# A two-block transformer forward pass on one core: GpSimd's tile arithmetic goes to VectorE, and two prices of the list scheduler change

## The chip, the cores and the metric

The program runs on one core of one Trainium2 chip. The metric is the device time of one execution in microseconds (us). Five engines of the core take part: TensorE (PE; its weight loads stand as PEld), VectorE (DVE), ScalarE (ACT), GpSimd (POOL) and SyncE (SP), whose queue issues the weight loads from HBM.

## The reference

512 tokens of width 1024 go through two blocks of two layers each, all in float32.

```python
def first_block(...):                      # DEPTH = 2
    for layer in range(DEPTH):
        g = norm_gains[layer]
        h = rmsnorm(x, g[0])
        x = x + 0.5 * rmsnorm(swiglu(h, w_ffn_gate[layer, 0], w_ffn_up[layer, 0], w_ffn_down[layer, 0]), g[1])
        h = rmsnorm(x, g[2])
        x = x + rmsnorm(token_mixer(h, ...), g[3])         # 16 heads: dilated, differential, stick-breaking
        h = rmsnorm(x, g[4])
        x = x + 0.5 * rmsnorm(swiglu(h, w_ffn_gate[layer, 1], ...), g[5])
    return x

def second_block(x, ...):
    for l in range(DEPTH):
        proj = x @ w_in[l]
        ...
        o_a = hgrn2_mixer(hq, hf, hi, hg, lbs[l], hg_norm_w[l])     # gated recurrence, 4 heads
        o_b = nsa_mixer(nq, ...)                                    # sparse attention, 8 heads
        mix = jnp.concatenate([o_a, o_b], axis=-1) @ w_out[l]
        x = layer_norm(ALPHA * x + mix, ln1_g[l], ln1_b[l])
        ffn = (jax.nn.silu(x @ w_ffn_gate[l]) * (x @ w_ffn_up[l])) @ w_ffn_down[l]
        x = layer_norm(ALPHA * x + ffn, ln2_g[l], ln2_b[l])
    return x
```

## The kernel before

**Matmuls.** Activations lie feature by token: `x` is eight tiles of 128x512. Every large product is made of rounded matmuls (the type fp32r): a float32 operand is split into a rounded part `hi` and a rest `lo = src - hi`, and three matmuls (hi by hi, hi by lo, lo by hi) are summed in PSUM. For weights, `weights` loads a `raw` tile by SP's queue and makes two `ws` tiles from it: the `copy` to `hi` may run on VectorE or ScalarE, the subtraction for `lo` is marked `either`. Activations go through `split` in the same way (tiles `h`, `gu`, `m`).

**Stages.** A feed-forward stage runs 22 units of gate and up products (`mm<-h,ws`), then the down product (`mm<-gu,ws`); a mixer runs its own projections, heads and an output product (`mm<-m,ws`). Each stage ends in a tail (`tail` in the first block, `tail_ln` in the second), whose last units are cut into two halves of 256 tokens. When a half's units are done, `post` makes the norm: column sums on TensorE (`nb<-ones,acc`), `rsqrt` as a chain of 12 small VectorE instructions on tiles `sm`, two transposes (`nb<-c_ident,sm`) that spread the result, then for each of the eight tiles `tc<-y,nb` and `x<-x,tc`. The next stage's preparation follows: `tc<-x,c_gains`, the split to `h`, and for the norm of `x` a square on ScalarE and sums `tc<-tc`. The six such passages of the first block, and four in the second, are called transitions here. While a half is normed, TensorE works on the other half's units, and its weights need `ws` tiles from the same helper engines.

**Order.** Nothing of the order is written by hand. `Recorder` records all instructions on logical tiles; a list scheduler with prices (`Op.price`, ns) and latencies (`LAT`) simulates the five engines, in 12 rounds forward and backward, and keeps the shortest. Then `issue` emits every instruction in that order, so that each engine's queue is fixed and all instructions carry the line of `issue`, L665. An instruction marked `either` has two forms, and the scheduler picks VectorE or GpSimd for each one as it goes; `copy` and `scale` have a VectorE and a ScalarE form. `either` stands only where both operands lie in SBUF (`split` names VectorE where its source is in PSUM). A few tiles are cleared by `nc.gpsimd.memset` whatever the marks say.

Of the kernel before, what the change touches and what calls it, by code (L numbers as in the profile page):

```python
# [26 lines left out]


class Buf:
    """A logical tile. Its slot and its Tile tile come when the order of instructions is known."""  # L30

    def __init__(self, parts, cols, dt, tag, name, dram=None):
        self.parts, self.cols, self.dt, self.tag, self.name, self.dram = parts, cols, dt, tag, name, dram
# [15 lines left out]


class V:
    """A view of a logical tile: partitions, and an access pattern over a partition's elements."""

    def __init__(self, buf, dt, p0, np_, off, dims, pstep=None, raw=None):
        self.buf, self.dt, self.p0, self.np, self.off, self.dims, self.raw = buf, dt, p0, np_, off, dims, raw
# [122 lines left out]
class Op:  # L178
# [3 lines left out]
    def __init__(self, idx, eng, meth, args, kw):  # L182
        self.idx, self.eng, self.meth, self.args, self.kw = idx, eng, meth, args, kw
        vs = [x for x in args if isinstance(x, V)]
        outs = []
        ins = []
        for i, x in enumerate(args):
            if isinstance(x, V):
                (outs if i == 0 or i == 3 and meth == "pair" else ins).append(x)
        for k, x in kw.items():  # L190
            if isinstance(x, V):
                (outs if k == "accum_out" else ins).append(x)
        self.outs, self.ins = outs, ins
        self.deps, self.users = {}, []
        self.bufs = list({id(v.buf): v.buf for v in outs + ins}.values())
        self.func = args[2] if meth == "activation" and args[2] in SETS else None
        self.prices = {}
        self.forms = {}
        if meth == "copy":
            forms = {"vector": ("tensor_copy", args, kw), "scalar": ("activation", args + (AF.Copy,), kw)}  # L200
        elif meth == "scale":
            out, src, by = args
            forms = {"vector": ("tensor_scalar", (out, src, by, None), {"op0": OP.mult}),
                     "scalar": ("activation", (out, src, AF.Copy), {"scale": by})}
        else:
            forms = {e: (meth, args, kw) for e in (("vector", "gpsimd") if eng == "either" else (eng,))}
        for e in forms:
            self.eng = e
            self.meth, self.args, self.kw = forms[e]
            self.price()  # L210
            self.prices[e] = self.cost
        self.forms = forms
        self.choose(next(iter(forms)))
# [5 lines left out]
    def price(self):  # L219
        m = self.meth  # L220
        out = self.outs[0] if self.outs else None
        n = out.count() if out is not None else 0
        vs = self.ins + self.outs
        psum = any(v.buf.tag in PSUM for v in vs)
        if self.eng == "tensor":
            lhs = self.ins[0]
            load = lhs.count() / 1.2
            if lhs.dt == F32R:
                self.busy = n / 2.4
                self.cost = max(n / 2.4 + 2.5, load)  # L230
            elif m == "transpose":
                self.busy = self.cost = 107
            elif m == "pair":
                self.busy = 4 * n / 2.4
                self.cost = self.busy + 110
            else:
                self.busy = 4 * n / 2.4
                self.cost = max(self.busy + 2, 2 * load if n > 8 or n == 1 else load)
        elif self.eng == "sync":
            self.cost = max(475, vs[0].count() * vs[0].np / 90.0)  # L240
        elif self.eng == "scalar":
            self.cost = (52 if psum else 94) + n / 1.2 + (187 if "accum_out" in self.kw or isinstance(self.kw.get("bias"), V) else 0)
        elif self.eng == "gpsimd":
            self.cost = 90 + {"memset": 1.0, "tensor_copy": 3.5}.get(m, 2.22) * n
        else:
            ptr = any(v.count() == 1 for v in self.ins[1:])
            if m in ("tensor_copy", "tensor_scalar", "memset") and not psum:
                self.cost = 65 + n / 1.92 + (64 if ptr else 0)
            elif m == "reciprocal":
                self.cost = 65 + 8 * n / 0.96  # L250
            elif m == "tensor_tensor_reduce" or m == "tensor_reduce":
                self.cost = 75 + self.ins[0].count() / 0.96
            else:
                self.cost = 70 + n / 0.96 + (60 if psum and m == "scalar_tensor_tensor" else 0)
# [19 lines left out]


class Recorder:
    """Records instructions on logical tiles, orders them by a list scheduler, and issues them in that order."""

    def __init__(self, nc, tc, ctx, plan):
        self.bass_nc, self.tc, self.ctx, self.plan = nc, tc, ctx, plan  # L280
# [105 lines left out]
        return out  # L386

    def backward(self):
        """Schedules the reversed instructions, those that ended last first; the starts in forward time."""
        ops = self.ops  # L390
        engines = ("tensor", "scalar", "vector", "gpsimd", "sync")
        ready = {e: [] for e in engines}
        idle = {e: True for e in engines}
        left = [len(op.users) for op in ops]
        freed = [()] * len(ops)
        for b in self.bufs:
            if b.slot is not None and b.prior is not None and b.opener is not None:
                freed[b.opener] += tuple(b.prior.members)
                for i in b.prior.members:
                    left[i] += 1  # L400
        at = [0.0] * len(ops)
        late = [0.0] * len(ops)
        events = []
        for op in ops:
            if left[op.idx] == 0:
                heapq.heappush(ready[op.eng], (-op.end, op.idx))
        now, done = 0.0, 0
        while done < len(ops):
            for e in engines:
                if idle[e] and ready[e]:  # L410
                    i = heapq.heappop(ready[e])[1]
                    idle[e] = False
                    heapq.heappush(events, (now + ops[i].cost, 0, i))
            now, kind, i = heapq.heappop(events)
            op = ops[i]
            if kind:
                heapq.heappush(ready[op.eng], (-op.end, i))
                continue
            idle[op.eng] = True
            done += 1  # L420
            late[i] = -now
            for d in op.deps:
                left[d] -= 1
                at[d] = max(at[d], now + LAT[ops[d].eng][op.eng])
                if left[d] == 0:
                    heapq.heappush(events, (at[d], 1, d))
            for d in freed[i]:
                left[d] -= 1
                at[d] = max(at[d], now + (2000 if ops[d].eng == "sync" else 180))
                if left[d] == 0:  # L430
                    heapq.heappush(events, (at[d], 1, d))
        return late
# [1421 lines left out]
```

## Time and profile before

| | before |
|---|---|
| device time, median of 3 runs | 3787.7 us (3786.96 to 3789.73) |
| span of the profiled execution | 3776.2 us |
| median less that span | 11.5 us |
| mean granted TensorE clock | 0.978 of full speed |
| PE busy | 3631.1 us (96% of the span) |
| DVE, ACT, POOL busy | 2241.1, 1699.6, 1078.0 us |

The profiled execution has no clocked time of its own beside its span: it runs from the first to the last instruction, 3776.2 us, and the timed runs come out 11.5 us longer, which is start and end outside the span. The busy time of an engine is the union of its instructions' durations. The granted clock is 1.00 at 2.4 GHz and 0.50 at 1.2 GHz.

### The profile page before, as it was taken

To read this page: it belongs to the slowest core of one execution; us is meant where nothing else is said; L and a number is where in the kernel's file an instruction comes from. 1 tells how busy PE (TensorE), PEld (TensorE's weight loads), DVE (VectorE), ACT (ScalarE), POOL (GpSimd) and SP (SyncE) were. 2 spreads that over 40 slices of the span, in tenths; PEclk is the share of its full clock that TensorE was granted. 3 is DMA by queue.
4 is the path that set the end of the run, shared out by engine and by line. 5 is a ranking of instruction groups with operands and counts; after the bars stand their busy time and mean duration, and the time that the engine had idled before them with its cause. 6 is when DMAs were issued, how large, how long until landed. Compare 5 with 4: busy or idle time off the path is not lost.

```text
span 3776.2 us, 56593 instructions
## 1 busy us (share of the span) xinstructions
PE 3631.1 (96%) x20836; PEld 3016.9 (80%) x20836; DVE 2241.1 (59%) x4611; ACT 1699.6 (45%) x3550; POOL 1078.0 (29%) x999
## 2 busy tenths in 40 slices
PE   8999899999999999899899999999999999999998
PEld 7878877778898889767788897668888977678888
DVE  7443787764367545886844384677333766674335
ACT  5333456543344334565433354465332555654324
POOL 3220422443224211522633042334111333232112
PEclk9999999999999999999999999899999999999999
DMA  5224422232353224312322452013323531123234
GB/s 165 95 93 133 157 81 76 96 112 95 95 150 124 95 92 144 130 59 74 125 98 93 118 173 93 29 32 123 112 95 102 172 98 51 40 90 129 95 90 139
DMA packets 121622, 393.08 MB, mean 104 GB/s; under 512 B 14813, under 2 KB 20102, under 8 KB 121345
## 3 DMA queue, kind: packets, MB, share of 16 engines
q1 hardware_dynamic: 121344, 389.47, 32.6%
q8 instruction: 164, 2.69, 0.3%
q14 instruction: 114, 0.93, 0.1%
HBM read 384.65 MB, written 4.77 MB: 103 GB/s over the span
## 4 chain that ended last, share of the span: by engine, by line
PE 47%; DVE 6%; issue 1%; ACT 1%; POOL 0%; DMA 0%; ACTq 0%; DVEq 0%; POOLq 0%; SPq 0%
PE mm L665 38%; PE at L665 4%; PE ah L665 2%; PE pv L662 2%; DVE ws L665 1%; PE ah L662 1%; DVE sm L665 1%; DVE tc L665 1%; DVE hw L665 1%; DVE h L665 1%; DVE x L665 0%; PE nb L665 0%; ACT ws L665 0%; POOL ws L665 0%; ACT L659 0%
## 5 line engine op out<-in xcount | busy, mean ns | idle before, releaser
L665 PE MATMUL mm<-h,ws 128*128 128x512 f32 (+1 forms) x9792 | 2102.3, 362 | 53.9 <-DVE ws L665 16.9
L665 PEld LDWEIGHTS mm<-h,ws 128*128 128x128 f32 x9792 | 1645.8, 192 | 357.8 <-issue 25.1
L665 ACT ACTIVATE ws<-raw 128x512 fp32r<-128x512 f32 (+1 forms) x1283 | 782.0, 616 | 1417.8 <-PE mm L665 1370.8
L665 POOL TENSOR_TENSOR ws<-raw,ws 128x512 fp32r<-128x512 f32 (+1 forms) x506 | 654.5, 1295 | 2061.6 <-ACT ws L665 1592.3
L665 DVE TENSOR_TENSOR ws<-raw,ws 128x512 fp32r<-128x512 f32 (+2 forms) x926 | 682.3, 741 | 798.6 <-ACT ws L665 732.1
L665 PE MATMUL mm<-gu,ws 128*128 128x256 f32 (+1 forms) x4752 | 813.0, 323 | 11.9 <-DVE ws L665 7.3
L665 PEld LDWEIGHTS mm<-gu,ws 128*128 128x128 f32 x4752 | 692.2, 191 | 90.5 <-DVE ws L665 12.9
L665 DVE TENSOR_TENSOR te<-te,mm 128x256 f32<-128x256 f32 (+1 forms) x228 | 98.8, 460 | 279.9 <-PE mm L665 275.2
L665 PE MATMUL mm<-ws,h 128*128 128x256 f32 (+1 forms) x1344 | 254.9, 303 | 1.7 <-DVE sm L665 0.7
L665 PE MATMUL mm<-m,ws 128*128 128x256 f32 (+1 forms) x1248 | 218.3, 321 | 7.5 <-DVE ws L665 7.2
L665 PEld LDWEIGHTS mm<-ws,h 128*128 128x128 f32 x1344 | 203.2, 195 | 14.7 <-issue 6.3
L665 PEld LDWEIGHTS mm<-m,ws 128*128 128x128 f32 x1248 | 175.6, 195 | 32.3 <-issue 12.4
L665 ACT ACTIVATE row<-row,sm 128x512 f32<-128x512 f32 (+2 forms) x267 | 148.3, 572 | 58.2 <-DVE sm L665 57.2
L665 ACT ACTIVATE gu<-te 128x256 fp32r<-128x256 f32 (+1 forms) x210 | 89.5, 452 | 129.8 <-DVE te L665 118.4
L665 DVE TENSOR_TENSOR te<-te,rt 128x256 f32<-128x256 f32 x157 | 119.4, 792 | 0.5
L665 DVE CAST ws<-raw 128x512 fp32r<-128x512 f32 x149 | 97.7, 656 | 33.2 <-PE mm L665 27.7
L665 DVE TENSOR_TENSOR te<-mm,rt 128x256 f32<-128x256 f32 x176 | 67.8, 419 | 81.7 <-PE mm L665 80.4
L665 POOL TENSOR_TENSOR hw<-hw 128x256 f32<-128x256 f32 x106 | 88.7, 846 | 92.9 <-ACT hw L665 80.0
L665 PE MATMUL at<-c_ident,row 128*128 128x128 f32 x528 | 114.4, 286 | 0.4 <-DVE sm L665 0.3
L665 DVE TENSOR_TENSOR gu<-te,gu 128x256 fp32r<-128x256 f32 (+1 forms) x159 | 94.2, 611 | 30.3 <-ACT gu L665 26.0
L665 DVE CUSTOM_DVE_ANT_0 row<-at,T 128x128 f32<-128x128 f32 (+1 forms) x180 | 88.8, 509 | 25.6 <-PE at L665 23.6
L665 ACT ACTIVATE hw<-hw 128x256 f32<-128x256 f32 (+2 forms) x181 | 75.5, 456 | 55.1 <-DVE hw L665 28.1
(249 smaller groups left out, 3429.7 us busy)
## 6 DMA issues: line engine op xcount, KB each, us to landing
raw<-in_wg_dram SPq DMA_DIRECT2D x156, 512.0 KB, 3.3
raw<-in_wu_dram SPq DMA_DIRECT2D x156, 512.0 KB, 3.2
raw<-in_wd_dram SPq DMA_DIRECT2D x144, 512.0 KB, 3.5
raw<-in_wd_dram SPq DMA_DIRECT2D x72, 384.0 KB, 3.2
raw<-in_wout_dram SPq DMA_DIRECT2D x52, 512.0 KB, 3.3
raw<-in_w_f_dram SPq DMA_DIRECT2D x52, 512.0 KB, 3.4
raw<-in_win_f_dram SPq DMA_DIRECT2D x44, 512.0 KB, 3.3
raw<-in_win_v_dram SPq DMA_DIRECT2D x20, 512.0 KB, 3.2
```

The costliest lines, as they stand in the source:

```text
L662: nc.tensor.matmul(*args[0:3], **kw)
L665: r = getattr(getattr(nc, op.eng), op.meth)(*args, **kw)
```

## The change

The diff in its core (three comment strings are dropped as well, without a change of line numbers):

```diff
@@ Op.__init__ @@
         else:
-            forms = {e: (meth, args, kw) for e in (("vector", "gpsimd") if eng == "either" else (eng,))}
+            forms = {e: (meth, args, kw) for e in ("vector" if eng == "either" else eng,)}
@@ Op.price @@
             if lhs.dt == F32R:
                 self.busy = n / 2.4
-                self.cost = max(n / 2.4 + 2.5, load)
+                self.cost = max(n / 2.4 + 13, load)
...
         elif self.eng == "scalar":
-            self.cost = (52 if psum else 94) + n / 1.2 + (187 if "accum_out" in self.kw or isinstance(self.kw.get("bias"), V) else 0)
+            self.cost = (62 if psum else 106) + n / 1.2 + (187 if "accum_out" in self.kw or isinstance(self.kw.get("bias"), V) else 0)
```

An `either` instruction now has a VectorE form alone. A rounded matmul of 512 columns is priced at 226.3 ns in place of 215.8, one of 256 columns at 119.7 in place of 109.2, and a ScalarE instruction at 10 or 12 ns more. Prices set the order and the choice between VectorE and ScalarE, and no instruction's work.

In the two programs TensorE has 19692 instructions before and now, and SP 857. GpSimd goes from 1004 to 42, VectorE from 4613 to 5431, ScalarE from 3312 to 3451. Of the 962 instructions that leave GpSimd 471 are the `lo` of a 128x512 weight tile. In exchange 92 of the 145 copies `ws<-raw` that VectorE made go to ScalarE.

VectorE's queue in the transition after layer 1's mixer (the fifth of the first block, 1790 to 1860 us in the trace), from the last step of the first half's `rsqrt` on. Before:

```order
L665 SCALAR_TENSOR_TENSOR sm<-sm 128x2 x2
L665 TENSOR_TENSOR tc<-y,nb 128x256 x3
L665 TENSOR_TENSOR x_70<-x_70,tc 128x256
L665 TENSOR_TENSOR tc<-y,nb 128x256 x2
L665 TENSOR_TENSOR x_72<-x_72,tc 128x256
L665 TENSOR_TENSOR x_78<-x_78,tc 128x256
L665 TENSOR_TENSOR tc<-y,nb 128x256 x3
L665 TENSOR_TENSOR x_88<-x_88,tc 128x256
```

The same place now:

```order
L665 SCALAR_TENSOR_TENSOR sm<-sm 128x2 x2
L665 TENSOR_TENSOR ws<-raw,ws 128x512
L665 TENSOR_TENSOR acc<-acc,te 128x256
L665 TENSOR_TENSOR tc<-y,nb 128x256 x2
L665 TENSOR_TENSOR x_72<-x_72,tc 128x256
L665 TENSOR_TENSOR tc<-y,nb 128x256
L665 TENSOR_TENSOR x_74<-x_74,tc 128x256
L665 TENSOR_TENSOR x_70<-x_70,tc 128x256
L665 TENSOR_TENSOR tc<-y,nb 128x256 x2
L665 TENSOR_TENSOR x_78<-x_78,tc 128x256
L665 TENSOR_TENSOR x_76<-x_76,tc 128x256
L665 TENSOR_TENSOR tc<-y,nb 128x256 x2
```

All eight `x<-x,tc` of the half now stand in VectorE's queue, where four did, and a weight tile's `lo` and a sum `acc<-acc,te` stand between the end of `rsqrt` and the first `tc<-y,nb`.

GpSimd's queue at the same place before (`x_...` are residual tiles, `ws` weights, `h` the next stage's input):

```order
L665 TENSOR_TENSOR ws<-raw,ws 128x512 x2
L665 TENSOR_TENSOR x_74<-x_74,tc 128x256
L665 TENSOR_TENSOR x_76<-x_76,tc 128x256
L665 TENSOR_TENSOR acc<-acc,te 128x256
L665 TENSOR_TENSOR x_84<-x_84,tc 128x256
L665 TENSOR_TENSOR x_94<-x_94,tc 128x256
L665 TENSOR_TENSOR ws<-raw,ws 128x512
L665 TENSOR_TENSOR acc<-acc,te 128x256
L665 TENSOR_TENSOR h<-tc,h 128x256 x2
```

GpSimd's queue now has nothing in the whole first block after its first clears; its rows from there on begin so:

```order
L665 MEMSET misc 128x64
L665 MEMSET mean 128x128
L665 MEMSET bd 128x256 x2
L665 MEMSET hw 128x512
L665 MEMSET hw 128x256
```

What moved is every subtraction, sum and product that GpSimd shared with VectorE; the clears stay.

## Rows read from the trace of the kernel before

**Rows 1.** The page's first part: busy us, share of the span, instructions.
```profile
PE 3631.1 (96%) x20836; PEld 3016.9 (80%) x20836; DVE 2241.1 (59%) x4611; ACT 1699.6 (45%) x3550; POOL 1078.0 (29%) x999
```

**Rows 2.** Windows: stretch, us, busy us of each engine, granted clock, DMA.
```profile
410.00:490.00 80.00, 66.64 (x505) 63.66 (x505) 74.39 (x156) 41.04 (x94) 42.43 (x38) 0.96 0.45 146
...
780.00:1100.00 320.00, 319.16 (x1623) 270.46 (x1622) 147.72 (x256) 120.65 (x230) 81.09 (x70) 1.00 0.35 110
...
1790.00:1860.00 70.00, 55.38 (x401) 52.59 (x400) 63.39 (x132) 35.86 (x81) 45.28 (x44) 0.90 0.35 114
...
2310.00:2420.00 110.00, 106.25 (x677) 81.92 (x676) 62.07 (x145) 49.66 (x114) 33.92 (x42) 0.83 0.17 56
```

**Rows 3.** The chain of waits from 1790 to 1860 us, shares by line.
```profile
by line: PE mm L665 24.4%; DVE tc L665 16.1%; DVE ws L665 12.7%; DVE sm L665 12.5%; issue 9.7%; DVE x L665 6.2%; DVE h L665 4.4%; PE nb L665 4.3%; DVE te L665 3.1%; POOL ws L665 1.9%; ACT tc L665 1.3%; ACT ws L665 1.3%; DVE acc L665 1.0%; D
```

**Rows 4.** VectorE's groups, 1790 to 1860 us: busy us, mean ns | idle before.
```profile
L665 DVE TENSOR_TENSOR ws<-raw,ws 128x512 fp32r<-128x512 f32 x16 | 13.4, 842 | 0.8 <-ACT ws L665 0.7
L665 DVE SCALAR_TENSOR_TENSOR sm<-sm 128x2 f32<-128x2 f32 x18 | 7.0, 387 | 0.6
...
L665 DVE TENSOR_TENSOR x<-x,tc 128x256 f32<-128x256 f32 x8 | 5.7, 720 | 0.0
L665 DVE TENSOR_TENSOR tc<-tc 128x256 f32<-128x256 f32 x7 | 5.4, 776 | 0.1
L665 DVE TENSOR_TENSOR h<-tc,h 128x256 fp32r<-128x256 f32 x10 | 5.4, 543 | 0.1
L665 DVE CAST ws<-raw 128x512 fp32r<-128x512 f32 x8 | 5.2, 650 | 0.9 <-PE mm L665 0.9
L665 DVE TENSOR_SCALAR tc<-x,c_gains 128x256 f32<-128x256 f32 x5 | 4.3, 869 | 0.0
L665 DVE TENSOR_TENSOR sm<-sm 128x2 f32<-128x2 f32 x10 | 3.4, 340 | 0.3
L665 DVE CAST h<-tc 128x256 fp32r<-128x256 f32 x5 | 3.1, 615 | 0.1
L665 DVE TENSOR_SCALAR sm<-sm 128x2 int32<-128x2 int32 x8 | 2.2, 278 | 0.2
```

**Rows 5.** GpSimd's largest group in the same stretch.
```profile
L665 POOL TENSOR_TENSOR ws<-raw,ws 128x512 fp32r<-128x512 f32 x16 | 21.7, 1360 | 11.2 <-ACT ws L665 6.7 <-DVE sm L665 3.0 <-DVE ws L665 1.0
```

**Rows 6.** VectorE's groups from 1400 to 1450 us, where GpSimd does nothing.
```profile
L665 DVE TENSOR_TENSOR ws<-raw,ws 128x512 fp32r<-128x512 f32 x18 | 12.5, 692 | 32.2 <-ACT ws L665 31.3 <-PE mm L665 0.9
```

**Rows 7.** Timeline near 1800 us: start us, length us, engine, instruction, count.
```profile
1799.36 0.16 DVE L665 TENSOR_TENSOR sm<-sm 128x2 f32<-128x2 f32 x1
1799.55 1.41 DVE L665 SCALAR_TENSOR_TENSOR sm<-sm 128x2 f32<-128x2 f32 x2
1799.64 1.30 POOL L665 TENSOR_TENSOR ws<-raw,ws 128x512 fp32r<-128x512 f32 x1 [0.55 <-ACT ws L665]
...
1803.74 1.08 DVE L665 TENSOR_TENSOR tc<-y,nb 128x256 f32<-128x256 f32 x3 [0.59 <-PE nb L665]
...
1812.17 0.28 DVE L665 CAST h<-tc 128x256 fp32r<-128x256 f32 x1
1812.48 0.42 DVE L665 TENSOR_TENSOR h<-tc,h 128x256 fp32r<-128x256 f32 x1
```

**Rows 8.** TensorE's waits over the span: total us, times, longest us.
```profile
PE mm L665 <- DVE ws L665: 31.3, 35, 5.2
PE nb L665 <- DVE sm L665: 27.9, 17, 3.8
```

**Rows 9.** Groups of the whole span: the products of the gated recurrence (hw).
```profile
L665 POOL TENSOR_TENSOR hw<-hw 128x256 f32<-128x256 f32 x104 | 85.4, 829 | 91.2 <-ACT hw L665 80.0 <-DVE hw L665 7.7 <-DVE sm L665 1.4
...
L665 DVE TENSOR_TENSOR hw<-hw 128x256 f32<-128x256 f32 x88 | 51.9, 605 | 9.2 <-ACT hw L665 6.5 <-POOL hw L665 2.4
```

**Rows 10.** TensorE's timeline in a feed-forward stretch.
```profile
849.73 25.57 PE L665 MATMUL mm<-h,ws 128*128 128x512 f32 x110
```

## The prediction

> **What bounds the kernel now.** I read the shares first. TensorE is busy for 96% of the span and GpSimd for 29% [rows 1], so only TensorE's 145 us without work (3776.2 - 3631.1), and what it loses to a low clock, are to be had. Next come the windows [rows 2]. In the feed-forward stretch from 780 to 1100 us TensorE is busy for 319 of 320 us while GpSimd works 81 us: what GpSimd does there is hidden, and will be hidden on VectorE too, which is busy for 148 of 320. In the transitions it is the other way round. From 1790 to 1860 us TensorE is idle for 14.6 of 70 us, the granted clock is 0.90, and VectorE is busy for 63.4. Five such stretches (410 to 490, 680 to 780, 1100 to 1170, 1510 to 1570, 1790 to 1860; the first and the last stand in the rows) hold 64 us of the 145.
>
> Then the chain of waits in that stretch [rows 3]: lines of DVE make up 56% of it, PE's matmuls 24%, GpSimd 2%. TensorE's own waits over the span say the same [rows 8]: 31.3 us for `ws` tiles that VectorE ends and 27.9 us for the `rsqrt` chain. So VectorE's queue paces the transitions, and the question is whether it becomes longer or shorter.
>
> Last, why VectorE is busy there. The reader is to compare one form in two places. A `ws<-raw,ws` of 128x512 takes 692 ns where GpSimd is silent [rows 6] and 842 ns in the transition [rows 4]. A step on 128x2 `sm` takes 0.16 us alone; two of them take 1.41 us when GpSimd's 1.30 us instruction starts 0.09 us behind them [rows 7]. The means in the transition, 387 and 340 ns for `sm`, 720 for `x<-x,tc`, 869 for `tc<-x,c_gains` [rows 4], are mixtures of clean and held-up ones. VectorE is held up by GpSimd, and GpSimd needs 1360 ns for what VectorE does in 692 [rows 5, 6].
>
> A page of the Trainium skill gives this a mechanism: "SBUF — State Buffer", section "SBUF: two separate sides", says that VectorE and GpSimd share one pair of SBUF ports as an exclusive lock, taken for a whole instruction by a GpSimd operation or by a VectorE one with two SBUF inputs or in a two-port mode. By that rule all held-up time goes with GpSimd's work, and the sum below would stand as it is. The trace agrees as far as the `sm` steps beside GpSimd's 1.30 us go.
>
> **The change, part by part: VectorE's load.** I work it out for 1790 to 1860 us.
>
> Held-up time that goes, count by mean [rows 4] less clean duration ([rows 6] for 512 columns, [rows 7] for the others; I take 0.42 us for every 256-column form and for the 512-column CAST, which is kind, since a 256-column CAST takes 0.28): `ws` 16 x (842 - 692) = 2.4 us; `sm` steps 18 x (387 - 160) = 4.1, 10 x (340 - 160) = 1.8, 8 x (278 - 160) = 0.9; `x` 8 x 300 = 2.4; `tc` 7 x 356 = 2.5; `h` 10 x 123 = 1.2; CAST of `ws` 8 x 230 = 1.8; `tc<-x,c_gains` 5 x 449 = 2.2; CAST of `h` 5 x (615 - 280) = 1.7. Sum 21.0 us.
>
> Work that comes: GpSimd has 44 instructions there [rows 2], 16 of them on 512 columns [rows 5], the other 28 on 256. In a queue without waits three 256-column instructions take 1.08 us, and one alone 0.42, so each more costs 0.33 [rows 7]. A 512-column one costs 0.69 less the same overlap of 0.09, so 0.60. 16 x 0.60 + 28 x 0.33 = 18.8 us.
>
> Work that leaves VectorE for ScalarE: the order after has none of the 8 CASTs of `ws` in this transition, 8 x 0.33 = 2.6 us. ScalarE is busy for 36 of 70 us there and takes them.
>
> Net: 63.4 - 21.0 + 18.8 - 2.6 = 58.6 us, so VectorE's queue is 4.8 us shorter although it has GpSimd's work too. Five transitions: **24 us**. If the chain were on VectorE for its 56% alone, 13; if all held-up time on it went and the moved work found gaps, up to TensorE's whole idle time in the five, 64.
>
> **The clock.** At 0.90 over 70 us TensorE ran 14 us at its lower level of 1.2 GHz (2 x 0.10 x 70) [rows 2], after pauses on VectorE. Over the span 0.978 makes 166 us at half speed, at most 83 us lost. Of that I give the transitions back **12 us**: fewer pauses, not none. Bounds: 0 and 83.
>
> **The gated recurrence.** From 2310 to 2420 us the clock is 0.83, 37 us at half speed [rows 2]. There products of `hw` stand between an exponential and small matmuls. GpSimd's 104 take 829 ns, VectorE's 88 take 605, a clean one 420 [rows 9, 7]: 104 x 0.41 + 88 x 0.19 = 59 us of latency shorter. TensorE has other matmuls to run meanwhile, so I let a quarter count: **15 us**. Bounds: 0 and 59.
>
> **The prices.** They change the order alone. 110 rounded matmuls of 512 columns take 25.57 us, 232 ns each [rows 10]; the old price was 215.8, the new one is 226.3. The old plan thus expected TensorE sooner than it came, and knew nothing of held-up instructions, so its order in the transitions fits the chip badly. The new plan errs less. The price of this I know from no row. In the feed-forward stretches TensorE has some 1 us of idle time in 320 [rows 2], so there is nothing to win and little to lose; in the transitions it may be worth as much as the held-up time, or cost it. I take **10 us** gained, bounds -20 and +40.
>
> **What may get worse on the path.** The first half's `rsqrt` now has a `ws` and an `acc` between its end and the first `tc<-y,nb`, 0.60 + 0.33 us; the queue was idle for 0.59 us there while TensorE made the transposes [rows 7], so 0.3 us are left, in a handful of places. A queue that holds everything also waits as one: while VectorE waits for ScalarE's `hi`, the `x` sums behind it wait too, which GpSimd did before. That belongs to the third rival. The 42 clears left on GpSimd cost nothing I can see.
>
> Sum: 24 + 12 + 15 + 10 = 61 us. The span becomes 3715 us. The median of the runs lies 11.5 us over the span, and I take this as unchanged: 3726 us, 1.6% faster.
>
> **Rivals.**
> 1. *Much faster.* The transitions' pauses come mostly from the held-up instructions and an order made for wrong prices; with both gone the clock stays up too. Half of the 145 us idle and half of the 83 us of clock: 114 us, 3674 us. For it: VectorE ends TensorE's two largest kinds of wait [rows 8]. Against: after the change VectorE still has 58.6 us to do in 70.
> 2. *No change.* The transitions are bound by the sequence of steps (sums, `rsqrt`, transposes, `tc`, `x`, `h`, `ws`) and not by load; each gain is lost to the next wait. Some 3780 to 3795 us. Against: single `sm` steps on that very sequence are held up for over 1 us.
> 3. *Slower.* In the transitions VectorE becomes the one queue that all work stands in. If all 18.8 us that come lie on the chain, and of the 21.0 us held-up time only its share of the chain, 56% or 12 us, goes, each of the five is 7 us longer; the second block's four, taken as equal to them, by as much: 9 x 7 = 63 us, 3850 us. It decides when VectorE is busy over 95% of a transition and the transition is longer than before. A rule of the Trainium skill speaks for it: "Perfetto Trace Analysis", section "Optimizing Scalar/DVE Operations", says that with a saturated VectorE it may make sense to give work to ScalarE or even to GpSimd, though it adds that between GpSimd and VectorE this may not help because of the shared port. The trace bears the addition out: in the transition 45 us of GpSimd's work are worth 18.8 us of VectorE's and cost it 21.0.
> 4. *The held-up time isn't GpSimd's doing*, so that it stays. Then VectorE needs 63.4 + 18.8 - 2.6 = 80 us for the 70, some 10 us more in each of the five, 3838 us or worse. Against: where GpSimd is silent 18 `ws` subtractions have a mean of 692 ns [rows 6], and none of the held-up `sm` steps in the timeline lacks a GpSimd instruction beside it [rows 7].
>
> **How the numbers follow.** My forecast, between 3690 and 3765 us, has a chance of 0.58; the first rival, below that, 0.19; the stretch from 3765 to 3780 us 0.07; no change 0.08; the third rival 0.06 and the fourth 0.02. The three runs of before spread over 2.8 us, so 0.2% (7.6 us) is about what can be told from no change. Faster: 0.58 + 0.19 + 0.07 = 0.84; same 0.08; slower 0.08. The range takes in the forecast and most of the first rival, down to 3650, where gains of more than 135 us would need nearly all pauses to vanish, and up to 3780; outside lie some 0.18.
>
> **What would show it.** Right: `ws<-raw,ws` of 128x512 at 690 ns everywhere and `sm` steps at 160; VectorE's busy time over the span near 2300 us in spite of 818 more instructions; TensorE's idle time down from 145 to about 100 us; a mean granted clock above 0.98; the feed-forward stretches as long as before. Wrong: long durations on VectorE that stay, or transitions in which VectorE is busy throughout and TensorE waits longer for `ws`. The prediction fails most easily where it is guessed: the clock, the recurrence, and the new order.

## The result and the profile after

The changed kernel takes 3663.5 us (median of 4 runs, 3658.43 to 3664.8) where the kernel before takes 3787.3 beside it: a ratio of 0.9669 (95% interval 0.9656 to 0.9683). The forecast was 3726: the sign was right, and the gain of 124 us is twice the 61 us of the sum. The first rival's 3674 is nearest. Medians here and below are of the executions at the usual clock: in two of the later kernels one execution of four, at a granted clock of 0.65, is left out.

Time and span lie 2.2 us apart here (3663.71 and 3661.5), and 1.7 to 2.3 us in every run for which both are known. So the 11.5 us by which the median of the kernel before lies over its profile's span are not start and end: that profile is of an execution of some 3778 us, 9 us quicker than the median. By the two spans the gain is 114.7 us, by the medians 123.8.

The page's first part of the changed kernel, the answer to [rows 1]; the span is 3661.5 us:

```profile
PE 3567.5 (97%) x20836; PEld 2984.1 (81%) x20836; DVE 2244.5 (61%) x5429; ACT 1752.7 (48%) x3689; POOL 10.7 (0%) x38
```

TensorE's idle time fell from 145.1 to 94.0 us (3661.5 - 3567.5), and VectorE is busy for as long as before with 818 more instructions, as the forecast said. The mean granted clock is 0.983.

VectorE's groups of the changed kernel in the same transition as [rows 4] (its place is now 1745 to 1817 us), and over the span the products of the recurrence, the answer to [rows 9]:

```profile
L665 DVE TENSOR_TENSOR ws<-raw,ws 128x512 fp32r<-128x512 f32 x31 | 21.1, 687 | 0.4
...
L665 DVE TENSOR_TENSOR x<-x,tc 128x256 f32<-128x256 f32 x16 | 6.2, 421 | 0.0
...
L665 DVE SCALAR_TENSOR_TENSOR sm<-sm 128x2 f32<-128x2 f32 x24 | 3.8, 160 | 0.8
```

```profile
L665 DVE TENSOR_TENSOR hw<-hw 128x256 f32<-128x256 f32 (+1 forms) x196 | 79.7, 423 | 9.7 <-ACT hw L665 9.2
```

Each of these is at the duration that the forecast called clean (842, 720, 387 and 605 ns before).

TensorE's waits over the span, the answer to [rows 8]:

```profile
PE nb L665 <- DVE tc L665: 43.0, 7, 12.3
PE mm L665 <- DVE ws L665: 17.3, 14, 7.0
...
PE nb L665 <- DVE sm L665: 5.1, 4, 2.4
```

The waits for `ws` and for the `rsqrt` steps are down from 31.3 and 27.9 us. What is late next is `tc`: seven waits, up to 12.3 us long, in which TensorE waits for VectorE's sums of squares `tc` for the next stage's norm. All of TensorE's waits in this view, those not shown here too, add up to 86 us in 38 waits; before it was 135 us in 134.

**Where the time went.** I cut all kernels at the same amount of matmul work (columns started by TensorE), so that a stretch holds the same work in each; for the kernel before the cuts are the first matmuls after the forecast's round times. The windows of the five transitions that the forecast summed, of the changed kernel (columns as in [rows 2]):

```profile
407.60:481.00 73.40, 65.98 (x506) 63.97 (x505) 69.03 (x183) 45.51 (x101) 0.00 (x0) 0.93 0.48 158
667.30:759.70 92.40, 78.98 (x571) 76.56 (x570) 73.58 (x200) 52.42 (x113) 0.00 (x0) 0.89 0.37 122
1077.70:1142.60 64.90, 55.66 (x447) 55.30 (x445) 57.43 (x163) 40.90 (x92) 0.00 (x0) 0.89 0.47 144
1480.30:1533.50 53.20, 46.26 (x354) 44.84 (x354) 51.38 (x137) 32.69 (x74) 0.00 (x0) 0.94 0.47 154
1745.20:1816.70 71.50, 58.83 (x402) 57.37 (x401) 59.79 (x179) 38.10 (x85) 0.00 (x0) 0.79 0.34 111
sum 355.40, PE 305.71 PEld 298.03 DVE 311.21 ACT 209.61 POOL 0.00; mean PE 61.14 PEld 59.61 DVE 62.24 ACT 41.92 POOL 0.00
```

The same five before:

```profile
411.70:490.10 78.40, 66.73 (x505) 63.75 (x506) 72.79 (x155) 40.32 (x92) 41.34 (x37) 0.96 0.44 144
680.20:780.10 99.90, 84.20 (x575) 78.05 (x574) 79.02 (x161) 49.44 (x104) 52.44 (x47) 0.91 0.35 115
1100.10:1170.10 70.00, 59.90 (x447) 57.34 (x446) 63.92 (x133) 36.76 (x82) 44.34 (x42) 0.93 0.42 134
1510.10:1570.10 60.00, 50.00 (x355) 46.99 (x354) 54.87 (x112) 31.38 (x71) 38.27 (x35) 0.91 0.41 136
1790.10:1860.10 70.00, 55.38 (x400) 52.59 (x399) 63.39 (x132) 35.76 (x80) 45.38 (x44) 0.90 0.35 114
sum 378.30, PE 316.20 PEld 298.71 DVE 334.00 ACT 193.67 POOL 221.79; mean PE 63.24 PEld 59.74 DVE 66.80 ACT 38.73 POOL 44.36
```

They are 22.9 us shorter, and VectorE's busy time in them by 22.8. The granted clock is lower than before in four of the five (0.79 in the last one, 0.90 before). The four mixer stretches, before and then after:

```profile
490.10:680.20 190.10, 186.88 (x1031) 134.43 (x1030) 148.84 (x357) 122.62 (x291) 42.02 (x35) 0.99 0.21 66
1570.10:1790.10 220.00, 214.32 (x1215) 158.41 (x1214) 167.61 (x379) 134.68 (x318) 56.77 (x45) 1.00 0.22 74
2170.00:2600.10 430.10, 417.04 (x2728) 329.95 (x2727) 289.95 (x676) 214.47 (x487) 142.42 (x151) 0.94 0.27 85
3060.20:3390.10 329.90, 317.95 (x2024) 236.23 (x2023) 219.09 (x565) 178.52 (x409) 108.64 (x115) 0.95 0.20 62
sum 1170.10, PE 1136.20 PEld 859.02 DVE 825.50 ACT 650.28 POOL 349.84; mean PE 284.05 PEld 214.75 DVE 206.38 ACT 162.57 POOL 87.46
```

```profile
481.00:667.30 186.30, 185.93 (x1035) 133.94 (x1034) 155.26 (x385) 126.03 (x301) 0.00 (x0) 1.00 0.21 67
1533.50:1745.20 211.70, 211.45 (x1214) 157.91 (x1214) 173.61 (x421) 139.93 (x327) 0.00 (x0) 1.00 0.23 76
2122.80:2517.10 394.30, 392.19 (x2729) 313.08 (x2728) 288.54 (x804) 223.80 (x505) 5.14 (x16) 1.00 0.29 92
2959.80:3278.60 318.80, 311.07 (x2018) 233.73 (x2017) 220.32 (x643) 182.04 (x427) 2.98 (x9) 0.96 0.21 63
sum 1111.10, PE 1100.64 PEld 838.66 DVE 837.72 ACT 671.80 POOL 8.12; mean PE 275.16 PEld 209.67 DVE 209.43 ACT 167.95 POOL 2.03
```

Here lie 59 us, half of the whole gain. TensorE's idle time falls from 33.9 to 10.5 us, and the time at 1.2 GHz from 88 us (2 x (0.01 x 190.1 + 0.06 x 430.1 + 0.05 x 329.9)) to 26 (2 x 0.04 x 318.8), which is worth 31 us.

The same cuts for the runs below, us in the profiled execution (an ordinary table, summed from the traces). Each row is one execution, and executions of one kernel differ (the kernel before: 3771.7 to 3793.1 us in ten), so a few us in one cell decide nothing:

```
                                        5 transitions  4 mixers  2nd block's   feed-    start  all
                                        of block 1               transitions   forward
before                                      378.2       1170.2     260.3       1904.8    60.0  3773.6
prices only, GpSimd kept                    381.1       1170.0     270.9       1907.0    62.6  3791.5
old order, all moved                        346.7       1157.0     255.4       1897.8    56.4  3713.2
old order, weight tiles moved               350.1       1153.2     255.9       1904.5    57.5  3721.2
old order, recurrence moved                 384.8       1165.1     259.6       1905.4    59.5  3774.4
planned without GpSimd, old prices          351.1       1121.6     244.0       1888.8    60.6  3666.2
the changed kernel                          355.3       1111.0     244.4       1886.4    61.7  3658.8
planned, GpSimd for all but weights         382.6       1145.1     259.1       1914.9    61.0  3762.6
planned, GpSimd for weights only            372.7       1130.5     260.3       1899.6    58.9  3722.1
planned, GpSimd at twice its price          366.1       1159.2     260.3       1910.5    64.8  3760.9
changed order, third weight on GpSimd       371.4       1123.3     251.0       1901.1    63.2  3710.0
changed, GpSimd busy until 1185 us          402.9       1131.4     244.5       1897.3    69.4  3745.5
```

### The profile page after: what moved, and what is told of

The parts are those of the page before. It is cut to its first block, busy times and chain, and to the rows that moved or that the text cites. A ratio compares the mean times of both kernels' runs of the same rounds, so it can differ in the third digit from the quotient of the medians.

```text
span 3661.5 us, 55849 instructions
## 1 busy us (share of the span) xinstructions
PE 3567.5 (97%) x20836; PEld 2984.1 (81%) x20836; DVE 2244.5 (61%) x5429; ACT 1752.7 (48%) x3689; POOL 10.7 (0%) x38
## 4 chain that ended last, share of the span: by engine, by line
PE 93%; DVE 5%; ACT 1%; issue 1%; DMA 0%; SPq 0%; ACTq 0%; DVEq 0%
PE mm L665 80%; PE at L665 6%; PE pv L662 2%; PE ah L665 2%; PE nb L665 2%; PE ah L662 1%; DVE tc L665 1%; DVE ws L665 1%; DVE x L665 1%; DVE sm L665 1%; DVE h L665 0%; ACT ws L665 0%; SPq L665 0%; DVE row L665 0%; PE pv L665 0%
## 5 line engine op out<-in xcount | busy, mean ns | idle before, releaser
L665 PE MATMUL mm<-h,ws 128*128 128x512 f32 (+1 forms) x9792 | 2076.1, 361 | 9.8 <-DVE ws L665 9.6
L665 ACT ACTIVATE ws<-raw 128x512 fp32r<-128x512 f32 (+2 forms) x1376 | 837.4, 616 | 1382.6 <-PE mm L665 1353.8
L665 DVE TENSOR_TENSOR ws<-raw,ws 128x512 fp32r<-128x512 f32 (+1 forms) x1432 | 955.7, 672 | 738.2 <-ACT ws L665 684.0
L665 PE MATMUL mm<-gu,ws 128*128 128x256 f32 (+1 forms) x4752 | 797.7, 320 | 0.3 <-ACT ws L665 0.2
L665 PE MATMUL mm<-ws,h 128*128 128x256 f32 (+1 forms) x1344 | 237.5, 293 | 0.5 <-ACT ws L665 0.2
L665 PE MATMUL at<-NK,NQ 128*128 128x256 f32 (+5 forms) x256 | 88.3, 393 | 0.0
L665 ACT ACTIVATE te<-te 128x256 f32<-128x256 f32 x176 | 70.4, 414 | 32.3 <-DVE te L665 32.3
L665 DVE TENSOR_TENSOR hw<-hw 128x256 f32<-128x256 f32 (+1 forms) x196 | 79.7, 423 | 9.7 <-ACT hw L665 9.2
L665 PEld LDWEIGHTS at<-c_ident,row 128*128 128x128 f32 x528 | 67.5, 141 | 18.9 <-issue 5.8
```

Source lines behind the costliest of these rows:

```text
L665: r = getattr(getattr(nc, op.eng), op.meth)(*args, **kw)
```

## The experiments

**The change taken apart.** Three kernels: without the new prices; with the new prices alone; and the plan of before, in which each instruction given to GpSimd is issued on VectorE at its place in the order.

```diff
@@ e1: Op.price, on the changed kernel @@
-                self.cost = max(n / 2.4 + 13, load)
+                self.cost = max(n / 2.4 + 2.5, load)
...
-            self.cost = (62 if psum else 106) + n / 1.2 + ...
+            self.cost = (52 if psum else 94) + n / 1.2 + ...
@@ e2: the same two lines the other way, on the kernel before @@
@@ e3: issue, on the kernel before @@
+                    eng = "vector" if op.eng == "gpsimd" and op.meth != "memset" else op.eng
-                    r = getattr(getattr(nc, op.eng), op.meth)(*args, **kw)
+                    r = getattr(getattr(nc, eng), op.meth)(*args, **kw)
```

> GpSimd's arithmetic goes to VectorE, the scheduler's prices stay as they were before. Theory H (held-up time: the 124 us come from VectorE instructions that GpSimd no longer holds up, whatever the order): at least 80 of the 124 us, 3705 us or less. Theory O (order: they come from a plan whose prices fit the chip): 30 us or less, 3757 us or more, since the prices of matmuls and ScalarE are the old ones; though the plan no longer counts on GpSimd, which helps O a little.

> Only the two prices change; GpSimd keeps its share of the arithmetic. Theory H: within 15 us of before (3787 us), as VectorE is held up as often. Theory O: at least 50 us faster, 3737 us or less, with TensorE's spacing of 256-column matmuls down from 120 ns to 117.

> The plan of before is kept to the letter, with GpSimd counted on; only when it is issued, each of GpSimd's 962 arithmetic instructions is put on VectorE's queue at the place of its planned start. Theory H: faster than before by 50 to 100 us (3690 to 3737 us), with a ws subtraction of 512 columns at 692 ns everywhere. Theory O: 3770 us or more, or slower than before, since VectorE's queue is now in an order that nobody planned.

Measured beside 3784.6 us of the kernel before: without the new prices 3670.1 us (ratio 0.9701, 0.9684 to 0.9718), the prices alone 3797.1 (1.0034, 1.0019 to 1.0049), the old order on VectorE 3716.5 (0.9824, 0.9803 to 0.9846). So the move alone, in an order made for two engines, is worth 68 us; planning without GpSimd 46.5 more; the prices 6.5 us (12 by the ratios) where there is no GpSimd to plan for, with intervals that all but touch. With GpSimd kept, the same prices cost 12.5 us. Theory O falls with the prices alone. Theory H has its numbers in the first and the third kernel, but not "whatever the order": the two differ by the plan.

The old order on VectorE in the five transitions:

```profile
405.80:481.50 75.70, 65.91 (x505) 62.50 (x506) 71.71 (x194) 40.65 (x93) 0.00 (x0) 0.98 0.48 155
672.40:760.80 88.40, 79.66 (x574) 74.17 (x573) 73.33 (x208) 49.24 (x104) 0.00 (x0) 0.96 0.38 128
1080.10:1143.90 63.80, 56.95 (x446) 54.66 (x445) 59.94 (x174) 36.19 (x82) 0.00 (x0) 0.97 0.45 146
1482.60:1539.00 56.40, 49.82 (x354) 45.90 (x353) 53.36 (x145) 31.71 (x71) 0.00 (x0) 0.94 0.43 139
1765.10:1827.50 62.40, 52.50 (x401) 50.11 (x400) 58.19 (x174) 35.85 (x80) 0.00 (x0) 0.95 0.39 127
sum 346.70, PE 304.85 PEld 287.34 DVE 316.53 ACT 193.63 POOL 0.00; mean PE 60.97 PEld 57.47 DVE 63.31 ACT 38.73 POOL 0.00
```

The clock is higher in all five (0.90 to 0.95 in the last one), and the five are 31.6 us shorter. The same kernel gained only 13 us in the mixers, and layer 1's mixer even became longer, 226 us against 220 before and 212 in the changed kernel. TensorE's largest waits in that mixer in the old order on VectorE (1539 to 1765 us), and all of them in the changed kernel:

```profile
PE at L666 <- DVE pt L666: 3.3, 4, 1.3
PE at L666 <- DVE sm L666: 1.6, 1, 1.6
PE mm L666 <- DVE Q L666: 0.9, 1, 0.9
PE mm L666 <- DVE V L666: 0.8, 1, 0.8
```

```profile
PE mm L665 <- DVE ws L665: 0.2, 1, 0.2
```

VectorE's longest wait there: before, in the old order on VectorE, and in the changed kernel:

```profile
DVE ws L665 <- ACT ws L665: 15.0, 9, 4.4
DVE ws L666 <- ACT ws L666: 14.8, 8, 4.4
DVE ws L665 <- ACT ws L665: 8.1, 6, 3.8
```

All of TensorE's waits in this mixer are 5.3 us before, 9.0 in the old order on VectorE and 0.2 in the changed kernel. Nearly all are for short copies and steps that VectorE ends late (`pt`, `sm`, `Q`, `V`), and in the plan made for one queue they are gone. It is tempting to say that the moved subtractions wait for ScalarE's `hi` and hold these copies up behind them. But VectorE waits as long for `hi` in the kernel before as in the old order on VectorE, so that this wait did not come with the move. The timeline shows work instead. VectorE, then TensorE, at one of these pauses in the old order on VectorE:

```profile
1593.98 1.21 DVE L666 TENSOR_TENSOR_SCAN ta<-ta,zeros 128x511 f32<-128x511 f32 x1
1595.11 0.67 DVE L666 TENSOR_TENSOR ws<-raw,ws 128x512 fp32r<-128x512 f32 x1
1595.69 0.68 DVE L666 COPY pt<-at 128x512 f32<-128x512 f32 x1
```

```profile
1596.52 0.36 PE L666 MATMUL at<-K,Q 128*128 128x256 f32 x1 [1.07 <-DVE pt L666]
```

In the 2.5 us ahead of the end of each of TensorE's ten pauses over 0.3 us in this mixer VectorE works without a break, and in seven of them a weight tile's subtraction of 0.7 us stands ahead of the copy that TensorE waits for. So the copies come late behind work in the one queue and not behind waits; which of these subtractions GpSimd had before isn't read here. The fresh plan differs in one more way than order: 92 of VectorE's 145 copies `ws<-raw` of 128x512 went to ScalarE, some 39 us of VectorE's time at 418 ns each. No run separates this from the order.

**Is it GpSimd's presence?** Additions of its own, for which nobody waits, are given to GpSimd in the changed kernel. In the first form they were issued ahead of the clears:

```diff
@@ e4 and e8: issue, on the changed kernel (e8: after the fourth clear) @@
+            for _ in range(N_PAD):                        # 1800
+                nc.gpsimd.tensor_tensor(pads[2][:, :], pads[0][:, :], pads[1][:, :], op=OP.add)
```

> The changed kernel, with 1800 additions of 128 columns on tiles of GpSimd's own, which nobody waits for, run without a pause from the start: some 0.4 us each, so to about 650 to 700 us of the span. Theory H: as long as they run, VectorE's subtractions and sums with two SBUF inputs take longer than 692 and 415 ns, those that read PSUM do not, and the first two transitions are longer than in the changed kernel; in all 20 to 60 us slower than it, 3684 to 3724 us; behind the last addition all is as in the changed kernel. Theory O: within 8 us of the changed kernel, 3663 us.

It took 4246.8 us (ratio 1.1236) and tells little of the time: a clear was queued behind the additions, and TensorE stood still until they had ended. So the second form puts them behind the first four clears.

> The changed kernel, and after its first four clears GpSimd makes 1800 additions of 128x128 on tiles of its own (505 ns each, so until about 910 us); nothing waits for them, and the next clear comes at 2163 us. Theory, GpSimd's mere presence holds VectorE up on the path: while they last, VectorE's 256-column instructions with two SBUF sources rise from 420 to some 680 ns, those with a PSUM source stay, the stretches up to 910 us grow by 30 to 80 us in all, and the time becomes 3695 to 3745. Rival, held-up time is hidden beside TensorE: the durations rise but the time stays at 3657 to 3671.

Measured: 3743.4 us (ratio 0.9899, 0.9881 to 0.9917), 80 us more than the changed kernel (87 by the ratios), at the upper end of the range. The rival falls. GpSimd's queue (start, length), VectorE's groups while the additions last, and the same groups from 1185 to 2200 us:

```profile
1.83 1182.83 POOL L677 TENSOR_TENSOR pad<-pad,pad 128x128 f32<-128x128 f32 x1800
```

```profile
L666 DVE TENSOR_TENSOR ws<-raw,ws 128x512 fp32r<-128x512 f32 x424 | 342.5, 813 | 144.3 <-ACT ws L666 135.9 <-PE mm L666 5.5
L666 DVE TENSOR_TENSOR gu<-te,gu 128x256 fp32r<-128x256 f32 x88 | 57.1, 679 | 0.5 <-ACT gu L666 0.5
...
L666 DVE TENSOR_TENSOR te<-te,mm 128x256 f32<-128x256 f32 x88 | 35.1, 418 | 97.6 <-PE mm L666 97.5
```

```profile
L666 DVE TENSOR_TENSOR ws<-raw,ws 128x512 fp32r<-128x512 f32 x393 | 268.6, 687 | 173.1 <-ACT ws L666 162.5 <-PE mm L666 5.4 <-issue 1.6
L666 DVE TENSOR_TENSOR gu<-te,gu 128x256 fp32r<-128x256 f32 x88 | 35.2, 419 | 2.8 <-ACT gu L666 0.5
L666 DVE TENSOR_TENSOR te<-te,mm 128x256 f32<-128x256 f32 x88 | 35.1, 418 | 118.2 <-PE mm L666 118.1
```

GpSimd's mere work lengthens VectorE's instructions with two SBUF sources from 419 to 679 ns and leaves those with a PSUM source (`te<-te,mm`) at 418. This agrees with the Trainium skill, "SBUF — State Buffer", section "SBUF: two separate sides", by which a GpSimd instruction that reads SBUF and a VectorE instruction with two SBUF inputs exclude each other for a whole instruction. GpSimd is held up too: in the first form an addition had a mean of 453 ns from 600 to 1000 us, where VectorE did nothing, and 571 until 420 us, where it worked; here the mean is 579. With the gaps between the additions (141 us in all) they lasted until 1185 us, not 910. Of the 87 us between the two profiled executions (3748.2 - 3661.5) 75 lie ahead of the end of the third transition, in which the additions end. The other 12 lie in the mixer of the second block's second layer, long after the additions; that stretch also differs by up to 9 us with GpSimd silent (last section).

> The changed kernel in its own order, but every third subtraction for a weight tile (477) is issued on GpSimd. If the hold on VectorE costs the same in either order: 58 us, 3722 (3705 to 3740). If the new order is as good for a shared GpSimd as for none, so that the order and not the hold carries the gain: 3660 to 3685.

```diff
@@ e16: issue, on the changed kernel @@
+                    lo = op.meth == "tensor_tensor" and op.outs[0].buf.tag == "ws"
+                    los += lo
-                    r = getattr(getattr(nc, op.eng), op.meth)(*args, **kw)
+                    r = getattr(getattr(nc, "gpsimd" if lo and los % 3 == 0 else op.eng), op.meth)(*args, **kw)
```

Measured: 3714.9 us (ratio 0.9822, 0.9805 to 0.9839), 51 us more (58 by the ratios), within the first range. So weight tiles on GpSimd cost about as much in the new order as in the old (59 us for 506 of them, below). The hold is not alone in this: TensorE also waits 14.1 us, in 33 waits, for tiles that GpSimd ends, which needs 1305 ns for each.

**Which work is the harm?** The plan of before, with parts of GpSimd's work issued on VectorE.

```diff
@@ e9, e10, e11: issue, on the kernel before @@
+                    move = op.eng == "gpsimd" and op.meth != "memset" and op.outs[0].buf.tag == "ws"
...                    (e10: tag == "hw"; e11: tag not in ("ws", "hw"))
+                    r = getattr(getattr(nc, "vector" if move else op.eng), op.meth)(*args, **kw)
```

> The order of before; of GpSimd's arithmetic only the 506 subtractions for weight tiles are issued on VectorE, the other 456 instructions stay. Theory A, GpSimd's busy time as such holds VectorE up: they are 654.5 of some 1065 us, so 0.61 of the 68 us that moving everything gave, 41 us: 3743 (3733 to 3753). Theory B, the chains through GpSimd's short links cost the time and the weight tiles lie in slack: 3775 to 3787.

> The order of before; only the 133 products and sums of the gated recurrence (hw) are issued on VectorE. The term of the prediction: 15 us, 3769 (3764 to 3774). Rival, the recurrence is all that the two mixers of the second block gained when everything was moved in the old order: 26 us, 3758 (3750 to 3763). Theory A (shares of GpSimd's busy time): 112 of 1065 us, 7 us, 3777.

> The order of before; all that is neither a weight tile nor the recurrence (some 320 sums, products and subtractions of the transitions, the feed-forward and the mixers) is issued on VectorE. Theory A: 300 of 1065 us, 19 us, 3765 (3757 to 3773). Theory B: 68 less the recurrence's share, 40 to 53 us, 3731 to 3744.

Measured beside 3785.5 us: weight tiles 3726.6 (0.9848, 0.9828 to 0.9868), recurrence 3778.4 (0.9975, 0.9964 to 0.9986), the rest 3780.5 (0.9982, 0.997 to 0.9993). So 59, 7 and 5 us, 71 in sum, against 68 for all at once. Both theories miss: by shares of busy time (A) the weight tiles would give 41, and by the short links (B) next to nothing; the rest, with the short links, gives 5. Only the recurrence is where theory A has it, at 7 us; the prediction's term was 15. Why the weight tiles weigh more than their share is not shown.

**Why does planning afresh gain?**

```diff
@@ e13, e14: Op.__init__, on the kernel before with the new prices @@
-            forms = {e: (meth, args, kw) for e in (("vector", "gpsimd") if eng == "either" else (eng,))}
+            forms = {e: (meth, args, kw) for e in ((("vector",) if outs[0].buf.tag == "ws" else ("vector", "gpsimd"))
+                                                    if eng == "either" else (eng,))}
...                    (e14: the two tuples changed round)
@@ e15: Op.price @@
-            self.cost = 90 + {"memset": 1.0, "tensor_copy": 3.5}.get(m, 2.22) * n
+            self.cost = (90 + {"memset": 1.0, "tensor_copy": 3.5}.get(m, 2.22) * n) * (1 if m == "memset" else 2)
@@ e12: the changed kernel, n / 2.4 + 11 in place of + 13 @@
```

> New prices, planned afresh: only the subtractions for weight tiles have VectorE alone, everything else marked either still has both engines; the plan then gives GpSimd 753 instructions of the other kinds. Theory W, the weight tiles on GpSimd are the harm, also in the plan: near the changed kernel, 3660 to 3695. Theory P, a plan that counts on GpSimd for anything loses its 46 us: 3700 to 3740.

> The mirror: new prices, planned afresh, the subtractions for weight tiles have both engines (the plan gives GpSimd 564 of them), everything else marked either has VectorE alone. Theory W: little is won, 3750 to 3795. Theory P: a loss between the two kernels, and no less than with the weight tiles on VectorE: 3710 to 3750.

> New prices, planned afresh with GpSimd's arithmetic at twice its price, so that the plan gives it 741 instructions, 442 of them weight tiles. If the harm is GpSimd's holding VectorE up, a dearer price takes away only what it takes off GpSimd: 3750 to 3790. If the harm is that the old plan counts on a GpSimd that is too quick, most of the gain comes back: 3680 to 3730.

> The changed kernel, the price of a rounded matmul raised by 11 ns in place of 13: another plan of the same kind, to see how far plans scatter. Theory, the 46 us between the two orders on VectorE come from planning without GpSimd and not from luck: 3655 to 3680. Rival, plans scatter by some tens of us and the change drew a good one: over 3685 or under 3645.

Measured: GpSimd for all but the weights 3767.7 us (0.9962, 0.9948 to 0.9976); for the weights only 3726.8 (0.9853, 0.9834 to 0.9873); at twice its price 3762.0 (0.9942, 0.9922 to 0.9962); the neighbouring price 3658.6 (0.9662, 0.9647 to 0.9677). Theory W falls in both half plans. Theory P does not fare much better: the first is slower than it has it, and the second lies in its range but is the faster of the two, which it ruled out. GpSimd's busy time does not set the loss either, 729 us in the first and 752 in the second. What the first plan has is more short instructions on GpSimd, 753 where the old plan had 456, and the table shows its loss in every kind of stretch but the start, the feed-forward ones too (1914.9 against 1886.4). Doubling the price gains 22 us by its ratio, within the first range. Three plans that count on GpSimd for nothing, with different prices, lie between 3658.6 and 3670.1 us, so the new plan is no lucky draw.

So it is shown that a plan without GpSimd gains 46.5 us over the old order when both run without it, and that plans that keep part of GpSimd's work keep part of the loss. In the half plans the hold and the order come together; none of them was run with GpSimd's share issued on VectorE. That a higher price does not bring the gain is presumably because the cost is paid in VectorE's instructions, which the planner prices as if alone; a planner that knows of the hold was not tried.

**The places in memory.** A tile's place follows the order of first use, so the change moved it too. In these kernels the tiles are given their places in a written order before the first instruction.

```diff
@@ e5, e6, e7, e17, e18: issue @@
+            for tag in PLACE.split():
+                real(first[tag])
```

> The changed kernel, its order of instructions untouched, but its tiles get the places in SBUF and PSUM of the kernel before (they follow the order of first use, which the change altered). Theory A, places set TensorE's pace: the 256-column rounded matmuls go back from a median of 118 ns to 120 and the time rises by 15 to 30 us to 3680 to 3693. Theory B, the order alone is worth the 46 us: the median stays at 118 and the time at 3657 to 3669.

> The old order with GpSimd's arithmetic issued on VectorE (3716.5 us), but the tiles get the places that the changed kernel gives them. Theory A, places: the median of the 256-column rounded matmuls falls from 120 to 118 ns and the time by 15 to 30 us, to 3686 to 3702. Theory B, order: 120 ns and 3709 to 3724.

> The changed kernel with the old places in SBUF and its own banks in PSUM. If places count (theory A) it stands with the run that takes both places back where SBUF decides (3680 to 3693), or with the changed kernel where PSUM's banks decide (3657 to 3669). Theory B: 3657 to 3669 whatever the places are.

> The changed kernel, its order untouched, with the places in memory of the half plan that kept only weight tiles on GpSimd (there 512-column rounded matmuls had a median of 227 ns and 256-column ones 120; in the changed kernel 231 and 118). If both paces go with the places: 8208 x 4 ns less 8736 x 2 ns is 15 us gained, 3648 (3640 to 3656). If places are worth nothing beyond the spread of runs: 3658 to 3670.

> The plan with the price of a rounded matmul raised by 11 ns (3658.6 us) with the same places: 3644 (3636 to 3652) if both paces go with the places, 3653 to 3665 if not.

Measured, with the medians from start to start of the rounded matmuls (counted over each trace):

```
                                  us       ratio    95% interval      512 columns  256 columns
before                            3787.3                                231 ns       120 ns
the changed kernel                3663.5   0.9669   0.9656 to 0.9683    231          118
 + old places                     3680.2   0.972    0.9698 to 0.9742    231          120
 + old places in SBUF alone       3670.5   0.9711   0.9689 to 0.9732    231          120
 + places of e14                  3654.0   0.9662   0.9646 to 0.9678    227          120
old order, all moved              3716.5   0.9824   0.9803 to 0.9846    231          120
 + new places                     3716.8   0.9827   0.9806 to 0.9849    232          118
neighbouring price (e12)          3658.6   0.9662   0.9647 to 0.9677    232          118
 + places of e14                  3650.6   0.9652   0.9638 to 0.9667    227          120
```

The pace goes with the places in SBUF, whatever the order. The price is small: 7 to 17 us for the old places in the new order (with both places as theory A has it, with SBUF alone between the theories), nothing for the new places in the old order (theory B), and 8 to 10 us (by the ratios 3 to 4) for those of e14. These last two lie in the ranges of "both paces go with the places", but their intervals overlap those of the same order without them, so the gain isn't shown. So of the 46 us between the two plans the places hold between nothing and some 17, and the plan itself holds the rest. The last kernel, 3650.6 us, is the fastest by its median; it isn't shown to be faster than the changed kernel.

## Why the prediction was half right

**Where it held.** Every form of VectorE's instructions in the rows of the changed kernel is back at its clean duration, so the fourth rival falls, and so does the second (no change). The move by itself went much as the first three terms have it: they make 51 us, and the old order on VectorE gained 68. In the five transitions load and clock were to give 24 + 12 = 36 us; that kernel gained 31.6. TensorE's idle time in them went from 62.1 to 41.9 us, and its time at 1.2 GHz from 59 to 27 us (twice the missing clock times the length, summed over the rows), which is worth 16. VectorE's busy time fell by 17.5 us there, by 22.8 in the changed kernel, where the sum has 24. The third rival (one queue for all) does not decide, as VectorE is busy for 84% of the last transition (59.79 of 71.50), under the 95% at which it was to; yet that transition did get 1.5 us longer, and layer 1's mixer 6 us in the old order.

**The step that failed** is the last term: "The prices. They change the order alone ... I take **10 us** gained, bounds -20 and +40." What it stands for gave 53 us: planning without GpSimd 46.5, the prices 6.5. Both its reason and its place were wrong. The reason was that the new prices fit the chip better; with GpSimd kept, the same prices cost 12.5 us, and what counts is that the plan has no GpSimd. The place was to be the transitions, with nothing to win elsewhere. From the old order on VectorE to the changed kernel the five transitions lost 9 us and the start 5, and the gain lies in the mixers (46 us), the second block's transitions (11) and the feed-forward stretches (11). In the four mixers the kernel before had 33.9 us of idle time and 88 us at 1.2 GHz, after waits too short to stand high in a list of waits. Why the fresh plan ends them is open: its order, or the copies that it gives to ScalarE.

**Other terms.** The clock's 12 us hold for the move alone. The fresh plan gives them back in the transitions (81 us at 1.2 GHz), where its pauses are fewer but longer: in the last one TensorE is idle for 5.3 and 7.0 us, and from within each of these pauses on it runs at 1.2 GHz for 17 and 14 us; before, the longest pause there was 5.2 us and the longest time at 1.2 GHz 7. The clock's gain in the changed kernel comes from the mixers. The gated recurrence's 15 us were 7 by themselves. The second block's transitions (15.9 us) and the feed-forward stretches (18.4 us of 1904.8) had no term; the move alone gave 4.9 and 7.0 of these.

**The first rival** came nearest in time and not by its working, so its nearness is luck: it took 72 us from idle time and 42 from the clock; by the two profiles they gave 51 and 21 (half of 2 x 0.022 x 3776 less 2 x 0.017 x 3662). The remaining 43 of 114.7 us lie in stretches that the profile counts as busy. Part of them may be the pace that goes with places, part presumably pauses too short to be seen between pipelined matmuls; how much of each stays open. Open is also why some places in SBUF are faster than others.

## What to carry to other kernels

Price a second engine by what it does to the first: 1.3 us of GpSimd's work on a weight tile saved VectorE 0.69 us, and taking it away made the kernel 59 us faster in an unchanged order. Sum idle time and clock by stage for every stage before judging an order: the mixers' short waits and the clock that they cost were worth more (59 us) than the longer waits of the transitions (23). To see what a planner's change is worth, run the new assignment in the old order first, and then the new plan.

## What the hardware showed unasked

GpSimd and VectorE hold each other up in both directions: an addition of GpSimd's took 571 to 579 ns beside a working VectorE, and 453 where VectorE did nothing. VectorE's sums of one SBUF and one PSUM source are exempt (418 ns with and without). Rounded matmuls run at 231 and 118 ns or at 227 and 120 ns for 512 and 256 columns, by the places of their tiles in SBUF. And the mixer of the second block's second layer differs with an unchanged order: 318.7 us in the changed kernel, 323.9 and 316.0 with the old places, 325.5 with those of e14, one execution each, so that places and chance aren't separated.
